# Moving the scaled input rows one block ahead and loading two sums one product sooner, in a two-layer encoder

## The chip, the core and the metric

The kernel runs on one core of one Trainium2 chip. A core has five engines that run side by side, each through its own list of instructions in order: TensorE (PE) multiplies matrices, VectorE (DVE) and ScalarE (ACT) work on tiles element by element, GpSimd (POOL) does a little arithmetic and issues DMAs, and SyncE (SP) only issues DMAs. DMAs move tiles between DRAM and the on-chip memory; those that add onto what is there already are issued by POOL here. The metric is the device time of one execution in microseconds (us); less is better. Times are medians of several executions.

## The reference

One sequence of 512 tokens of width 2048 goes through two layers in float32: attention with 16 query heads and 4 key/value heads, and a retention layer with 8 heads. What matters here are the large products with the weights and the residual.

```python
ALPHA = (2.0 * DEPTH) ** 0.25

def attention_mixer(h, w_in, q_gain, k_gain, w_out, cos, sin):
    proj = h @ w_in
    q, k, v, g = jnp.split(proj, [A_WIDTH, A_WIDTH + A_KV_WIDTH, A_WIDTH + 2 * A_KV_WIDTH], axis=-1)
    ...
    return (o * jax.nn.silu(g)) @ w_out

def retention_mixer(h, w_in, decay_exp, w_out, cos, sin):
    proj = h @ w_in
    q, k, v, g = jnp.split(proj, [R_QK_WIDTH, 2 * R_QK_WIDTH, 2 * R_QK_WIDTH + R_V_WIDTH], axis=-1)
    ...
    return (o * jax.nn.silu(g)) @ w_out

def reference(x, ...):
    for i in range(DEPTH):
        ...
        x = layer_norm(ALPHA * x + y, ln_gain[i], ln_bias[i])
    return x
```

## The kernel before

**Products.** A float32 product is made of three passes (`mm3`, L266 to L270): each operand is split into a rounded part and a remainder, and hi x hi, hi x lo and lo x hi are summed in PSUM. Weights come as chunks of 128 x 1024 values. One function, `split` (L116), makes the parts of a chunk: a cast on ACT (`whi`) and a subtraction on DVE (`wlo`). One chunk feeds twelve matmuls of 128 x 512 in the input blocks.

**Blocks.** The input projection of a layer is cut into blocks of 1024 columns, five in layer 1 (`a_in[0]` to `a_in[4]`, written block 0 to block 4 here) and twelve in layer 2 (`r_in`). Each block is a 2 x 2 product by Strassen's scheme, with seven products instead of eight; their numbers are 1 to 7, and the usual order is `ORDER` = 1, 5, 6, 3, 7, 2, 4. The weight side is cut into quarters B11, B12, B21, B22, and each product takes one sum of them, four chunks long. Those sums are formed in the raw tiles: `fetch` (L165) issues the load of a quarter on SP, `onto` (L145) adds another quarter by a DMA of POOL, and `make` (L183) adds two tiles on DVE: B22 for product 6 (L187), B21 for product 4 (L189). Product 5 needs B11 + B12. In an ordinary block that sum grows in the tile of product 1: once the chunk of product 1 is split, `follow` lets POOL add B12 onto it. In the blocks marked `first` (0 and 1 of each layer) products 1 and 2 stand far ahead, so `fetch` loads B11 again for product 5 and POOL adds B12.

**Order.** The first three blocks of a layer are interleaved as `LAYER_SEQ` says (block 0 products 1, 2; block 1 products 1, 2; block 0 products 5, 6, 3, 7; block 1 product 5; block 0 product 4; block 1 products 6, 3, 7; block 2 product 1; block 1 product 4; block 2 products 5, 6, 3, 7, 2, 4), then the others follow one by one. PE runs in exactly the order in which the code is written. The other engines' lists are put in order by the compiler's scheduler, except where `in_turn` ties instructions down. Chunks are split `AHEAD` = 2 ahead of PE and fetched `FETCH` = 3 ahead of that. A `hook` calls a function when PE's code reaches a given chunk of a given product of a block.

**Buffers.** Raw chunks live in a pool of 9 tiles (`rp`), and a load waits on SP until one is free. Split parts have 3 tiles each. A second pool, `xp`, has 32 tiles of the same size for the features, their sums and split forms, attention's operands and whatever needs a large buffer for long (`raw_load(..., large=True)`).

**Scaled rows.** The residual ALPHA * x goes into a DRAM tensor `yD`, onto which the output projection adds later. `residual_1` (L672 to L681) handles an eighth of it: SP loads 128 x 1024 values of x into an `xp` tile (L675), three chunks later ACT multiplies by ALPHA (L678) and POOL writes the tile to `yD` (L679). Its eight hooks stand in block 3 of layer 1 (L683 to L685), one in each of the seven products and a second in the fourth, product 3. Block 4 runs partly beside the start of attention, which reads keys, values, queries and gates back from DRAM.

Of the kernel before, what the change touches and what calls it, by code (L numbers as in the profile page):

```python
# [16 lines left out]
NT = S // P  # L17
# [26 lines left out]
ORDER = (1, 5, 6, 3, 7, 2, 4)  # L44

PAIR_SEQ = ((0, (1, 2, 5, 6, 3, 7)), (1, (1,)), (0, (4,)), (1, (5, 6, 3, 7, 2, 4)))
LAYER_SEQ = ((0, (1, 2)), (1, (1, 2)), (0, (5, 6, 3, 7)), (1, (5,)), (0, (4,)), (1, (6, 3, 7)), (2, (1,)), (1, (4,)),
             (2, (5, 6, 3, 7, 2, 4)))
# [5 lines left out]
def encoder_trunk_kernel(  # L54
# [33 lines left out]
    def nm(s):  # L88
        n_names[0] += 1
        return f"{s}{n_names[0]}"  # L90
# [4 lines left out]
    def x4(name, dt=F32R):  # L95
        return xp.tile([P, 1024], dt, tag="x", name=nm(name))
# [29 lines left out]
    def raw_load(src, large=False):  # L126
        raw = x4("raw", F32) if large else rp.tile([P, CH], F32, tag="raw", name=nm("raw"))
        x = nc.sync.dma_start(out=raw, in_=src)
        if fetched[0] < 12:
            in_turn(x)  # L130
        return raw

    def in_turn(x):

        tc.keep_in_program_order(x)
# [8 lines left out]
    def onto(x, src):  # L144
        return nc.gpsimd.dma_start(out=x, in_=src, accum_op=ALU.add)  # L145

    class Block:
# [17 lines left out]
        def fetch(self, p, c):  # L165
            q = lambda n: self.quarter(n, c)
            g = self.got
            if p == 1:
                g[1 if self.first else "v", c] = raw_load(q(11), self.hold)
            elif p == 2:  # L170
                g[2, c] = raw_load(q(21))
            elif p == 6:
                g[3, c] = raw_load(q(22), self.wide)
            elif p == 4 and self.again:
                g[2, c] = raw_load(q(21))
            elif p == 5 and self.first:
                if self.hold:
                    g["v", c] = g[1, c]
                else:
                    g["v", c] = raw_load(q(11))  # L180
                    onto(g["v", c], q(12))

        def make(self, p, c):  # L183

# [189 lines left out]
    def hook(blk, p, c, fn, *args):  # L374
        blk.hooks.setdefault((p, c), []).append(lambda: fn(*args))
# [150 lines left out]
    a_in = [Block(a["wa_in"][g], g < 2, hold=g == 0, again=g == 0, lean=g == A_G - 1) for g in range(A_G)]  # L526
    r_in = [Block(a["wr_in"][g], g < 2, again=g == 0) for g in range(R_G)]
# [47 lines left out]
    def form_hooks(ins, op):  # L575
        for (b, p, c), what in FORMS:
            hook(ins[b], p, c, op.form, *what)
# [102 lines left out]

        soon(3, scaled)  # L681

    for t in range(NT):  # L683
        for i in range(2):
            hook(a_in[3], ORDER[t + 3 * i], 1 + i, residual_1, t, i)  # L685

    cosq, sinq = [half(tabs, i).rearrange("p (t e) -> p t e", t=NT) for i in range(2)]

# [552 lines left out]
                x2.form(5, m // 2 % 2)  # L1241
    form_hooks(r_in, x2)
    hook(r_in[1], 6, 0, paused.clear)
    work.drain()


# [109 lines left out]
```

## Time and profile before

| what | value |
|---|---|
| median of 3 runs | 2105.22 us (2104.43 to 2105.92) |
| the profiled execution, its own time | 2108.04 us |
| its span from first to last instruction | 2106.2 us |
| granted clock of PE, mean | 0.998 |
| DMA, mean over the span | 186 GB/s, 390.80 MB |
| ACT, casts of `whi` (L117) | 644.7 us, 616 times |
| DVE, subtractions of `wlo` (L117) | 749.8 us, 616 times |
| SP waiting to load raw chunks (L128) until DVE has subtracted `wlo` | 524.6 us, 170 times |

In the profile, "out<-in" names the tile that an instruction writes and those that it reads; `raw` is a raw chunk, `acc` a sum in PSUM, `xs` a tile of scaled rows. "<-DVE wlo L117" at the end of a row says that the engine sat idle before it and that this ended the wait. PEld is the loading of weights into PE. A row of the chain of waits gives start, duration and what took the time; a DMA's duration runs from its issue to its landing. SP's rows are issues only: where two are merged, the duration runs from the first to the last.

### The profile page before, as it was taken

The page shows a single profiled execution, that of the slowest core. Times are in us where ns is not written, and L with a number is a line of the kernel's source. Part 1 is how long each engine was busy: PE and PEld are TensorE (multiplying, and loading weights), DVE is VectorE, ACT ScalarE, POOL GpSimd, SP SyncE. Part 2 cuts the span into 40 slices and gives each one's busy share as a digit, 9 for nine tenths or more (in the row PEclk, how much of TensorE's full clock was granted, in tenths as well). Part 3 has the DMA queues.
Part 4 walks back from the last instruction along what each step waited for, and adds up shares of the span by engine and source line. Part 5 has one row for each costly group of instructions (what it writes and reads, how often), then busy time and mean ns, then how long its engine had stood idle before and what let it go on. Part 6 is the DMA issues. An engine that isn't in the chain of part 4 may idle for free.

```text
span 2106.2 us, 26560 instructions
## 1 busy us (share of the span) xinstructions
PE 2084.9 (99%) x9684; PEld 1726.7 (82%) x9684; DVE 1611.2 (76%) x2153; ACT 1131.3 (54%) x1498; POOL 419.7 (20%) x507
## 2 busy tenths in 40 slices
PE   9999999999999999999999999999999999999997
PEld 7888887888888877888888888888888888888886
DVE  7888877889777878667786686666687888879666
ACT  6555556667643744444444444544466665666432
POOL 1144222122211112111211211211111122222100
PEclk9999999999999999999999999999999999999999
DMA  9776778457685868586786766566675587877762
GB/s 346 202 166 155 244 226 221 130 173 153 144 210 162 254 144 228 134 250 168 167 238 190 174 186 183 127 176 184 143 203 147 174 196 192 189 186 178 201 197 80
DMA packets 121971, 390.80 MB, mean 186 GB/s; under 512 B 14832, under 2 KB 17904, under 8 KB 121840
## 3 DMA queue, kind: packets, MB, share of 16 engines
q0 software_dynamic: 51040, 164.65, 38.0%
q1 hardware_dynamic: 70368, 223.53, 31.6%
q8 instruction: 76, 1.25, 0.2%
q10 hardware_dynamic: 432, 0.92, 0.1%
q14 instruction: 55, 0.45, 0.1%
HBM read 319.84 MB, written 69.21 MB: 185 GB/s over the span
## 4 chain that ended last, share of the span: by engine, by line
PE 88%; DVE 4%; DMA 4%; issue 2%; POOL 1%; ACT 1%; POOLq 0%; DVEq 0%; ACTq 0%
PE acc L269 25%; PE acc L270 25%; PE acc L268 25%; PE tr L522 3%; PE o L268 2%; PE o L269 2%; PE o L270 2%; PE s L268 1%; PE s L270 1%; PE s L269 1%; DVE wlo L117 1%; DMA raw<-in_wr_p_dram 1%; DMA raw<-in_wr_in_dram 1%; DMA raw<-in_wa_in_dram 1%; ACT whi L117 1%
## 5 line engine op out<-in xcount | busy, mean ns | idle before, releaser
L117 DVE TENSOR_TENSOR wlo<-raw,whi 128x1024 fp32r<-128x1024 f32 (+1 forms) x616 | 749.8, 1219 | 366.6 <-ACT whi L117 362.7
L117 ACT CAST whi<-raw 128x1024 fp32r<-128x1024 f32 (+1 forms) x616 | 644.7, 1050 | 665.5 <-PE acc L270 507.8
L268 PE MATMUL acc<-whi,f 128*128 128x512 f32 x2456 | 967.5, 394 | 1.5 <-ACT whi L117 1.5
L269 PE MATMUL acc<-wlo,f 128*128 128x512 f32 x2456 | 958.0, 390 | 6.6 <-DVE wlo L117 6.3
L270 PE MATMUL acc<-whi,f 128*128 128x512 f32 x2456 | 957.6, 390 | 0.0
L269 PEld LDWEIGHTS acc<-wlo,f 128*128 128x128 f32 x2456 | 461.7, 188 | 103.3 <-DVE wlo L117 12.0
L270 PEld LDWEIGHTS acc<-whi,f 128*128 128x128 f32 x2456 | 461.0, 188 | 96.9
L268 PEld LDWEIGHTS acc<-whi,f 128*128 128x128 f32 x2456 | 461.5, 188 | 94.6 <-ACT whi L117 3.0
L145 POOL DMA_DIRECT2D raw<-in_wr_in_dram x100 | 88.0, 880 | 396.4 <-DVE wlo L117 258.0
L187 DVE TENSOR_TENSOR raw<-raw,raw 128x1024 f32<-128x1024 f32 x86 | 105.1, 1227 | 2.3 <-DMA raw<-in_wa_in_dram 0.8
L386 ACT COPY t<-acc 128x512 f32<-128x512 f32 x150 | 84.8, 588 | 39.0 <-PE acc L270 35.0
L189 DVE TENSOR_TENSOR raw<-raw,raw 128x1024 f32<-128x1024 f32 x68 | 82.6, 1217 | 3.6 <-DMA raw<-in_wr_in_dram 3.6
L117 DVE TENSOR_TENSOR f<-xf,f 128x1024 fp32r<-128x1024 f32 (+2 forms) x67 | 78.1, 1171 | 9.1 <-ACT f L117 9.1
L117 ACT CAST f<-xf 128x1024 fp32r<-128x1024 f32 (+2 forms) x67 | 67.4, 1012 | 22.7 <-DMA xf<-in_xq_dram 5.8
L505 POOL TENSOR_TENSOR rstd<-rs_e,neg_half 128x1 f32<-128x1 f32 x40 | 31.3, 783 | 239.5 <-DVE rs_e L504 238.5
L145 POOL DMA_DIRECT2D raw<-in_wa_in_dram x48 | 42.7, 890 | 141.6 <-DVE wlo L117 111.3
L145 POOL DMA_DIRECT2D yD<-t x48 | 43.1, 986 | 117.9 <-DVE t L397 36.9
L1152 ACT ACTIVATE o<-o,nmr,rstd 128x512 f32<-128x512 f32 x32 | 24.9, 779 | 61.1 <-DVE nmr L516 61.1
L815 ACT ACTIVATE p<-s,nmax 128x512 f32<-128x512 f32 x64 | 44.1, 690 | 22.0 <-DVE s L813 17.1
L813 DVE TENSOR_SCALAR_CACHE_REDUCE s<-s,q_rs 128x512 f32<-128x512 f32 x64 | 48.0, 751 | 6.7 <-PE s L270 6.4
L268 PE MATMUL o<-inh,pTh 128*128 128x512 f32 x128 | 51.4, 401 | 0.0
L270 PE MATMUL o<-inh,pTl 128*128 128x512 f32 x128 | 50.0, 391 | 0.0
(205 smaller groups left out, 2200.0 us busy)
## 6 DMA issues: line engine op xcount, KB each, us to landing
raw<-in_wr_in_dram SPq DMA_DIRECT2D x156, 512.0 KB, 5.0
raw<-in_wr_in_dram POOLq DMA_DIRECT2D x100, 512.0 KB, 6.4
raw<-in_wa_in_dram SPq DMA_DIRECT2D x66, 512.0 KB, 6.2
raw<-in_wa_in_dram POOLq DMA_DIRECT2D x48, 512.0 KB, 7.6
raw<-in_wr_p_dram SPq DMA_DIRECT2D x36, 512.0 KB, 4.9
yD<-t POOLq DMA_DIRECT2D x48, 256.0 KB, 6.9
raw<-in_wr_p_dram POOLq DMA_DIRECT2D x24, 512.0 KB, 7.6
y<-yD SPq DMA_DIRECT2D x16, 512.0 KB, 6.5
```

The lines of the kernel that those rows point to most:

```text
L117: x, y = nc.scalar.copy(hi, src), nc.vector.tensor_sub(lo, src, hi.bitcast(F32))
L145: return nc.gpsimd.dma_start(out=x, in_=src, accum_op=ALU.add)
L187: nc.vector.tensor_add(v, v, g[3, c])
L189: x = nc.vector.tensor_add(v, v, g[2, c])
L268: nc.tensor.matmul(ps, sh, mh, start=start, stop=False, skip_group_check=go_on)
L269: nc.tensor.matmul(ps, sh, ml, start=False, stop=False, skip_group_check=go_on)
L270: nc.tensor.matmul(ps, sl, mh, start=False, stop=stop, skip_group_check=go_on)
L386: nc.scalar.copy(keep[p, t], bk[CHAIN[p]][t])
L505: nc.gpsimd.tensor_tensor(out=dst, in0=e[:, :n], in1=neg_half[:, :n], op=ALU.pow)
L522: nc.tensor.transpose(out=b[:, tcols(i)], in_=src[:, tcols(i)], identity=ident)
L813: nc.vector.tensor_scalar(sb, sb, rs, None, op0=ALU.mult, op1=ALU.min, accum_out=nmax)
L815: nc.scalar.activation(pt, sb, AF.Exp, scale=-1.0, bias=nmax, accum_out=self.sm[t][:, h:h + 1])
```

## The change

The first part hangs the eight calls of `residual_1` on block 2 of layer 1 (its last six products, 24 chunks, a call every third chunk) and no longer on block 3. The second part gives the load of B11 and the add of B12 for product 5 a function of its own, which does nothing where the sum is already asked for, and calls it for chunks 0 and 1 of layer 2's block 1 at the first two chunks of block 0's product 6, with large buffers out of `xp`.

```diff
@@ -177,8 +177,12 @@
                 if self.hold:
                     g["v", c] = g[1, c]
                 else:
-                    g["v", c] = raw_load(q(11))
-                    onto(g["v", c], q(12))
+                    self.fetch_sum(c)
+
+        def fetch_sum(self, c, large=False):
+            if ("v", c) not in self.got:
+                self.got["v", c] = raw_load(self.quarter(11, c), large)
+                onto(self.got["v", c], self.quarter(12, c))
 
@@ -680,9 +684,9 @@
-    for t in range(NT):
-        for i in range(2):
-            hook(a_in[3], ORDER[t + 3 * i], 1 + i, residual_1, t, i)
+    slots = [(p, c) for p in LAYER_SEQ[-1][1] for c in range(4)]
+    for n in range(2 * NT):
+        hook(a_in[2], *slots[3 * n], residual_1, n % NT, n // NT)
 
@@ -1241,6 +1245,8 @@
     hook(r_in[1], 6, 0, paused.clear)
+    for c in range(2):
+        hook(r_in[0], 6, c, r_in[1].fetch_sum, c, True)
     work.drain()
```

The number of instructions of every kind stays, and PE's list stays as it is. Source lines behind L178 move down by four, at the very end by six. Three places show what moves.

On POOL, at the head of block 4 of layer 1: the raw tiles are block 4's first four chunks, onto which B12 is added, `gD` and `qD` take gates and queries of block 3. Before:

```order
L679 DMA yD<-xs_2554 128x1024
L776 DMA qD_89<-qkT_2641 128x512
L505 TENSOR_TENSOR q_rs<-rs_e_2677,neg_half 128x4
L145 DMA raw_2581<-in_wa_in_dram 128x1024
L145 DMA raw_2611<-in_wa_in_dram 128x1024
L769 DMA gD_93<-gt_2711 128x512
L769 DMA gD_93<-gt_2714 128x512
L776 DMA qD_89<-qkT_2724 128x512
L145 DMA raw_2634<-in_wa_in_dram 128x1024
L679 DMA yD<-xs_2673 128x1024
L145 DMA raw_2666<-in_wa_in_dram 128x1024
```

and now:

```order
L780 DMA qD_89<-qkT_2645 128x512
L509 TENSOR_TENSOR q_rs<-rs_e_2679,neg_half 128x4
L145 DMA raw_2587<-in_wa_in_dram 128x1024
L145 DMA raw_2617<-in_wa_in_dram 128x1024
L773 DMA gD_93<-gt_2713 128x512
L773 DMA gD_93<-gt_2716 128x512
L780 DMA qD_89<-qkT_2726 128x512
L145 DMA raw_2638<-in_wa_in_dram 128x1024
L145 DMA raw_2670<-in_wa_in_dram 128x1024
```

The seventh and eighth write of scaled rows no longer stand ahead of and between the four adds.

On SP, in block 2 of layer 1: the first four raw tiles are its chunks of B22, those behind them its B21 for product 2. Before, no load of x stood here; the first came eight loads further on. Now:

```order
L128 DMA raw_1481<-in_wa_in_dram 128x1024
L128 DMA raw_1512<-in_wa_in_dram 128x1024
L679 DMA xs_1518<-in_x_dram 128x1024
L128 DMA raw_1537<-in_wa_in_dram 128x1024
L128 DMA raw_1557<-in_wa_in_dram 128x1024
L679 DMA xs_1596<-in_x_dram 128x1024
L679 DMA xs_1675<-in_x_dram 128x1024
L679 DMA xs_1750<-in_x_dram 128x1024
L128 DMA raw_1780<-in_wa_in_dram 128x1024
L128 DMA raw_1810<-in_wa_in_dram 128x1024
L679 DMA xs_1816<-in_x_dram 128x1024
L128 DMA raw_1834<-in_wa_in_dram 128x1024
```

Four loads of x go out among the chunks of B22, and the fifth stands between the second and third chunk of B21; it takes the buffer of the first, and so waits until that one's write has landed.

On DVE, where layer 2 goes from block 1's product 5 to block 0's product 4: rows of L189 add B21 for block 0's product 4 (`raw_6765`, `raw_6795`, `raw_6814`, `raw_6838` are its chunks 0 to 3), rows of L187 add B22 for block 1's product 6, and the `wlo` rows split a chunk. Before:

```order
L393 TENSOR_TENSOR t_6968<-t_6968,acc_6452 128x512
L189 TENSOR_TENSOR raw_6765<-raw_6765,raw_7190 128x1024
L117 TENSOR_TENSOR wlo_7217<-raw_7148,whi_7216 128x1024
L117 TENSOR_TENSOR wlo_7235<-raw_7167,whi_7234 128x1024
L189 TENSOR_TENSOR raw_6795<-raw_6795,raw_7214 128x1024
L117 TENSOR_TENSOR wlo_7254<-raw_6765,whi_7253 128x1024
L117 TENSOR_TENSOR wlo_7273<-raw_6795,whi_7272 128x1024
L189 TENSOR_TENSOR raw_6814<-raw_6814,raw_7232 128x1024
L189 TENSOR_TENSOR raw_6838<-raw_6838,raw_7250 128x1024
L117 TENSOR_TENSOR wlo_7296<-raw_6814,whi_7295 128x1024
```

and now (L193 and L191 are the old L189 and L187):

```order
L193 TENSOR_TENSOR raw_6765<-raw_6765,raw_7190 128x1024
L117 TENSOR_TENSOR wlo_7217<-raw_7148,whi_7216 128x1024
L193 TENSOR_TENSOR raw_6795<-raw_6795,raw_7214 128x1024
L117 TENSOR_TENSOR wlo_7235<-raw_7167,whi_7234 128x1024
L193 TENSOR_TENSOR raw_6814<-raw_6814,raw_7232 128x1024
L117 TENSOR_TENSOR wlo_7254<-raw_6765,whi_7253 128x1024
L193 TENSOR_TENSOR raw_6838<-raw_6838,raw_7250 128x1024
L191 TENSOR_TENSOR raw_6975<-raw_6975,raw_7269 128x1024
L117 TENSOR_TENSOR wlo_7273<-raw_6795,whi_7272 128x1024
L191 TENSOR_TENSOR raw_6995<-raw_6995,raw_7292 128x1024
L191 TENSOR_TENSOR raw_7148<-raw_7148,raw_7311 128x1024
L117 TENSOR_TENSOR wlo_7296<-raw_6814,whi_7295 128x1024
```

The additions of B21 for chunks 1 to 3 stand one or two places sooner, between the splits, and three additions of B22 now stand ahead of the split of chunk 2 of product 4 (`wlo_7296`). On POOL, the adds onto the two large buffers and onto chunk 2 of the sum (`raw_7148`) stand ahead of block 0's four adds for product 7; only chunk 3's stands behind them.

## The prediction

> **What bounds the kernel.** The order of views was: the page, PE's timeline, the chain of waits, the windows, then the timelines of SP and POOL and their waits.
>
> ```profile
> span 2106.2 us, 26560 instructions
> PE 2084.9 (99%) x9684; PEld 1726.7 (82%) x9684; DVE 1611.2 (76%) x2153; ACT 1131.3 (54%) x1498; POOL 419.7 (20%) x507
> ```
>
> PE is busy all the time, and the change leaves its instructions and their order as they are. So the only time to win is where PE stands still for operands, and the only time to lose is a new such place. I went through PE's timeline for starts that lie further apart than usual. Two groups hold most of what is lost after the start-up. The first is at the head of block 4 of layer 1:
>
> ```profile
> 337.19 0.39 PE L270 MATMUL acc<-whi,f 128*128 128x512 f32 x1
> 337.42 0.45 PE L268 MATMUL acc<-whi,f 128*128 128x512 f32 x1
> ...
> 338.97 0.39 PE L270 MATMUL acc<-whi,f 128*128 128x512 f32 x1
> ...
> 341.04 0.39 PE L270 MATMUL acc<-whi,f 128*128 128x512 f32 x1
> 342.50 0.50 PE L268 MATMUL acc<-whi,f 128*128 128x512 f32 x1 [1.07 <-ACT whi L117]
> 343.76 0.50 PE L269 MATMUL acc<-wlo,f 128*128 128x512 f32 x1 [0.76 <-DVE wlo L117]
> 344.10 0.40 PE L270 MATMUL acc<-whi,f 128*128 128x512 f32 x1
> ```
>
> The usual step from start to start is 0.23 (337.19 to 337.42). I count starts, since the ends are modelled. 337.42 to 338.97 are two steps that took 1.55 instead of 0.45, so 1.10 is lost; 341.04 to 342.50 loses 1.46 - 0.23 = 1.23; 342.50 to 344.10 loses 1.60 - 0.45 = 1.15. Together **3.48 us**. The second group is where layer 2 goes from its block 1, product 5, to block 0, product 4:
>
> ```profile
> 787.55 0.39 PE L270 MATMUL acc<-whi,f 128*128 128x512 f32 x1
> 788.35 0.50 PE L268 MATMUL acc<-whi,f 128*128 128x512 f32 x1 [0.41 <-ACT whi L117]
> ...
> 789.95 0.40 PE L270 MATMUL acc<-whi,f 128*128 128x512 f32 x1
> ...
> 800.78 0.39 PE L268 MATMUL acc<-whi,f 128*128 128x512 f32 x1
> 803.03 0.50 PE L269 MATMUL acc<-wlo,f 128*128 128x512 f32 x1 [1.87 <-DVE wlo L117]
> 803.37 0.39 PE L270 MATMUL acc<-whi,f 128*128 128x512 f32 x1
> ```
>
> Here 0.80 - 0.23 = 0.57, 1.60 - 0.45 = 1.15 and 2.59 - 0.45 = 2.14 are lost, together **3.86 us**. Both groups wait for a split whose raw chunk came late; the chain of waits says why.
>
> ```profile
> 326.16 15.14 DMA raw<-in_wa_in_dram
> ```
>
> **Part 1, the scaled rows.** The add of B12 into block 4's fourth chunk takes 15.14 us and lands at 341.30; PE gets the cast at 342.50 and the remainder at 343.76. The table of windows (busy us by engine, then granted clock, DMA share, GB/s) says why it takes so long:
>
> ```profile
> 300.00:305.00 5.00, 5.00 (x26) 4.13 (x25) 5.00 (x6) 2.96 (x4) 0.65 (x2) 1.00 0.45 150
> 305.00:310.00 5.00, 5.00 (x24) 4.13 (x23) 5.00 (x7) 2.19 (x3) 0.49 (x1) 1.00 0.95 302
> ...
> 335.00:340.00 5.00, 4.23 (x19) 3.14 (x18) 2.61 (x3) 1.57 (x2) 0.00 (x0) 1.00 1.04 302
> ```
>
> The 16 DMA engines are full from 305 to 340, so whatever leaves this stretch lets all that stands behind it land earlier by its service time. Three transfers of the scaled rows are in it, the eighth load and the last two writes (timelines of SP and POOL); the page's queue lines follow.
>
> ```profile
> 306.75 0.49 SPq L675 DMA_DIRECT2D xs<-in_x_dram  x1
> 314.63 0.54 POOL L679 DMA_DIRECT2D yD<-xs  x1
> ...
> 324.27 1.18 POOL L679 DMA_DIRECT2D yD<-xs  x1
> ```
>
> ```profile
> q0 software_dynamic: 51040, 164.65, 38.0%
> q1 hardware_dynamic: 70368, 223.53, 31.6%
> ```
>
> The queue lines give the service time of 512 KB (0.524 MB). On SP's queue it is 0.316 x 2106.2 x 0.524 / 223.53 = 1.56 us. On POOL's, mostly adds, it is 2.55 us; a plain write has no row of its own, so I bound it by these two. Sum: 1.56 + 2 x (1.56 to 2.55) = 4.7 to 6.7 us off the backlog. What is needed: without stall the chunk's second matmul would start at 341.04 - 1.10 + 2 x 0.23 = 340.4. It started at 343.76, so the landing has to come 3.4 us sooner, and 4.7 covers that. The chunk before needs 1.0 us, which the write at 314.63 gives alone. After it the attention's matmuls spread the chunks out, so nothing is near. I take 3.4 of the 3.48.
>
> The Trainium skill (DMA: Bandwidth & Descriptors, Queues, rings and completion order) says that each DMA engine takes turns between the queue rows, packet by packet. By it the load on SP's queue would delay POOL's adds by less than its service, and the two writes alone would count in full. The sum would then be 3.1 to 5.1 us against the 3.4 needed, and up to 0.3 of stall would stay. The 15.14 us of an add in a full stretch agrees with shared engines, but no row here separates the two queues' turns.
>
> The work itself is not saved. Eight loads, eight multiplies and eight writes now run in block 2. What covers them (SP's timeline, the windows, the multiply's own line):
>
> ```profile
> 169.36 0.33 SPq L128 DMA_DIRECT2D raw<-in_wa_in_dram  x1
> ```
>
> ```profile
> 170.00:180.00 10.00, 10.00 (x48) 8.31 (x47) 10.00 (x14) 6.17 (x8) 5.60 (x2) 1.00 0.25 90
> ...
> 200.00:210.00 10.00, 10.00 (x48) 8.28 (x47) 5.77 (x7) 5.01 (x6) 2.19 (x3) 1.00 1.03 215
> 210.00:220.00 10.00, 10.00 (x46) 8.29 (x45) 9.73 (x17) 4.39 (x6) 2.26 (x2) 1.00 0.53 186
> ```
>
> ```profile
> L678 ACT ACTIVATE xs<-xs x8: 1047/1057/1073, 252.6 to 322.2; 128x1024 f32<-128x1024 f32 x8
> ```
>
> In SP's new order the first load stands behind block 2's second chunk of B22 and three more behind the fourth, which goes out at 169.36; all four have a free buffer. Three of them thus fall into the window with a share of 0.25, and their 4.7 us fill it less than half. A multiply takes 1.06 us of ACT, which idles 4 to 6 us in ten here, and there is one in three chunks. The fifth to seventh load and the third to fifth write meet 200 to 220, full in its first half and half free in its second: 3 x 1.56 + 3 x (1.56 to 2.55) = 9.4 to 12.3 us of service against 4.7 free there. What does not fit, up to 7.6 us, moves on behind 220, where five of these loads no longer come. Chunks may land a few us later, but PE waits nowhere in this stretch now (10.00 of 10 in these rows). I price it at 0, and at rival (d) if the cover fails.
>
> **Part 2, B11 + B12 sooner.** The chain there:
>
> ```profile
> 774.64 7.55 DMA raw<-in_wr_in_dram
> ...
> 784.59 1.20 DVE t L393 x2
> 785.78 1.15 DVE raw L189
> ...
> 786.94 6.05 DMA raw<-in_wr_in_dram
> ...
> 795.41 5.19 DMA raw<-in_wr_in_dram
> ```
>
> Two things are late. First the adds of B12, of which the one at 774.64 is the second chunk's: these give the 0.57 and 1.15. Second, behind them, the loads of B21 for block 0's product 4: they need a raw buffer, and one is freed only when DVE has added the one before (L189, 785.78), so load and addition alternate until the last addition lets the split go that PE gets at 803.03 (the 2.14). With two chunks in large buffers the first changes at once: their loads need only a buffer that PE's transposes of the layer norm gave up.
>
> ```profile
> 734.35 0.33 SPq L128 DMA_DIRECT2D raw<-in_wr_in_dram  x1
> ```
>
> ```profile
> 745.00:755.00 10.00, 10.00 (x46) 8.29 (x45) 10.00 (x10) 5.74 (x7) 0.00 (x0) 1.00 0.00 0
> ```
>
> Their loads should go out right behind the one at 734.35, and their adds are done before 755, where the DMA share is 0.00 now; this costs nothing. The third chunk's load takes the place the first had. The fourth goes one freed buffer earlier, one chunk time of 12 x 0.23 = 2.7 us, and off the crowded stretch. So all four sums should be there before PE's turn: 1.72 us saved.
>
> For the second: the loads of B21 for chunks 0 to 2 now find free buffers as product 7 gives them up; only chunk 3 waits for L189. Product 7's last matmul is two chunks before the one at 787.55, at 787.55 - 2 x 2.7 = 782.1; L393 twice (1.20) and L189 (1.15), no longer held until 784.59, then end near 785.0 instead of 786.9, and chunk 3's load lands at 785.0 + 5.19 to 6.05 = 790.2 to 791.1 instead of 800.6. What is late next is the row of additions of B22 (L187) that DVE's new order puts ahead of the split: their loads go out as L189 and a split free buffers, at about 787.3, 789.6 and 790.8. The third lands at 796.0 to 796.9; addition and split (1.15 to 1.2 each) end at 798.4 to 799.3. PE, rid of 1.72, wants that split at 800.78 - 1.72 + 0.23 = 799.3 and, rid of smaller steps too, some tenths sooner. So 0 to 0.4 stays; I take 0.2. Part 2 gives 3.86 - 0.2 = 3.66, about 3.7.
>
> **Sum.** 3.4 + 3.7 = 7.1 us of the profiled execution (2108.0 us, 2.8 above the median). The stalls are no property of that one run, so I take them off the median: 2105.2 - 7.1 = **2098.1 us**.
>
> **Rivals.**
> (a) The backlog at 305 to 340 shrinks too little: only the last write, 1.56 us, counts for the late add. Then 3.4 - 1.56 = 1.8 stays: 2099.9. For it: the load and the first write were issued 19 and 12 us before the add. Against: the windows show no pause in between.
> (b) The buffers go on alternating and the 2.14 stays, as if a load took ten us: 2100.2. Against: the load moves by ten.
> (c) The change doesn't do what it says: the adds stay late because POOL or DMA fills the same way elsewhere, under 1 us is won: 2105.
> (d) Slower: SP blocks. In block 3 the fifth load waited 25.1 us for a write to free its buffer (SP's waits):
>
> ```profile
> SPq L675 <- DMA yD<-xs: 25.1, 1, 25.1
> ```
>
> ```profile
> 207.73 0.33 SPq L128 DMA_DIRECT2D raw<-in_wa_in_dram  x1
> ```
>
> ```profile
> 180.42 0.58 ACT L773 COPY qkT<-tr 128x512 f32<-128x512 f32 x1
> ```
>
> ```profile
> DMA to landing us min/median/max: 2.9/7.3/13.8
> ```
>
> In block 2 it comes behind the load at 207.73, ahead of two of product 2's loads and of block 3's. SP asks for a chunk five chunks ahead of PE (AHEAD + FETCH), 13.6 us, of which landing, cast and split take some 7.5 by the rows above. So SP may stand there until about 217; each us beyond costs one. Blocked for 25.1 us, to 233, it costs 16: 2105.2 - 7.1 + 16 = 2114. The change turns into a loss from 224 on. Against: the first write now follows its multiply, which stands right behind the copy at 180.42, and even with the slowest landing, 13.8, it is there by 196.
>
> **How the numbers follow.** Forecast 0.58 (2097.1 to 2099.5), (a) 0.14, (b) 0.10, (c) 0.11, (d) 0.07. The low end is the full 7.34 off, less the half span of the three runs (0.75). The high end, 2102.5, takes in (a) and (b) with twice their remainder; left out are (c) and (d), 0.18. A measurement of this kernel can tell 0.2%, 4.2 us, from no change: faster than 2101.0 are the forecast and most of (a) and (b), 0.76; slower 0.07; the rest 0.17.
>
> **What would show it.** Right: no gap over 0.3 us on PE around 335 to 345; the add that took 15.14 us lands in under 12; the eight loads between 162 and 230 with no SP wait of 10 us; two loads near 735; the first L189 about 2 us sooner, its last about 9. Wrong: a PE gap between 165 and 260, an ACT wait at the multiply, or a new wait for L187 where L189's was.

## The result, and the profile after

The changed kernel takes **2099.16 us** (median of 7 runs, 2098.53 to 2101.55). The kernel before, run beside it, takes 2105.78 us (7 runs, 2104.43 to 2108.82). The ratio is **0.9973, interval 0.9964 to 0.9982**: 5.7 us less, between 3.8 and 7.6. (The two medians lie 6.6 apart, which is inside that interval.)

The page of the changed kernel (busy us, share of the span, instructions):

```profile
span 2098.7 us, 26552 instructions
PE 2083.2 (99%) x9684; PEld 1726.7 (82%) x9684; DVE 1611.3 (77%) x2153; ACT 1133.2 (54%) x1498; POOL 419.5 (20%) x507
```

The span is 7.5 us shorter (2106.2 before), with the same 9684 matmuls. PE's timeline at the head of block 4 of layer 1 (start, duration, engine, line, operation), first before, then after:

```profile
334.70 0.39 PE L268 MATMUL acc<-whi,f 128*128 128x512 f32 x1
...
351.16 0.39 PE L268 MATMUL acc<-whi,f 128*128 128x512 f32 x1
```

```profile
334.70 0.39 PE L272 MATMUL acc<-whi,f 128*128 128x512 f32 x1
...
337.42 0.39 PE L272 MATMUL acc<-whi,f 128*128 128x512 f32 x1
337.65 0.41 PE L273 MATMUL acc<-wlo,f 128*128 128x512 f32 x1
...
340.22 0.39 PE L272 MATMUL acc<-whi,f 128*128 128x512 f32 x1
340.56 0.50 PE L273 MATMUL acc<-wlo,f 128*128 128x512 f32 x1
...
347.98 0.39 PE L272 MATMUL acc<-whi,f 128*128 128x512 f32 x1
```

Both pieces run from the first matmul of product 5's second chunk to the first of product 6's second. 57 steps lie between, and 334.70 to 337.42 gives 2.72 / 12 = 0.2267 for a step, so 12.92 us without a stall. Before it took 16.46, after 13.28: the **loss went from 3.54 to 0.36 us**, and no step is over 0.35 us. I use this "loss at block 4" for every run below.

In layer 2, from the first chunk of block 1's product 5 to the second of its product 6, 108 steps or 24.48 us without a stall, before and after:

```profile
782.34 0.39 PE L268 MATMUL acc<-whi,f 128*128 128x512 f32 x1
...
811.34 0.39 PE L268 MATMUL acc<-whi,f 128*128 128x512 f32 x1
```

```profile
779.26 0.39 PE L272 MATMUL acc<-whi,f 128*128 128x512 f32 x1
...
803.74 0.39 PE L272 MATMUL acc<-whi,f 128*128 128x512 f32 x1
```

29.00 before, 24.48 after: the **loss in layer 2 went from 4.52 to 0**. Together that is 3.18 + 4.52 = 7.7 us. Some of it was given back elsewhere, in block 6 of layer 2 (ACT's timeline, the two kernels after one another; a bracket names the wait that ended):

```profile
1181.50 2.01 ACT L117 CAST whi<-raw 128x1024 fp32r<-128x1024 f32 x2 [1.95 <-DMA raw<-in_wr_in_dram]
```

```profile
1175.05 2.94 ACT L117 CAST whi<-raw 128x1024 fp32r<-128x1024 f32 x3 [3.72 <-DMA raw<-in_wr_in_dram]
```

PE is 7.7 us ahead there, but this cast only 6.45 (1181.50 to 1175.05). PE had no time to spare at it before and lost 0.05 us in the six chunks around it; after, it lost 1.37. The change touches nothing in that block; the last section comes back to it.

### The profile page after: what moved, and what is told of

Its sections match the earlier page's. It is cut to its first block, busy times and chain, and to the rows that moved or that the text cites. A ratio compares the mean times of both kernels' runs of the same rounds, so it can differ in the third digit from the quotient of the medians.

```text
span 2098.7 us, 26552 instructions
## 1 busy us (share of the span) xinstructions
PE 2083.2 (99%) x9684; PEld 1726.7 (82%) x9684; DVE 1611.3 (77%) x2153; ACT 1133.2 (54%) x1498; POOL 419.5 (20%) x507
## 4 chain that ended last, share of the span: by engine, by line
PE 78%; issue 12%; DVE 3%; DMA 3%; POOL 2%; ACT 1%; POOLq 0%; DVEq 0%; SPq 0%; ACTq 0%
PE acc L273 22%; PE acc L274 22%; PE acc L272 22%; PE tr L526 3%; PE o L272 2%; PE o L274 2%; PE o L273 2%; DMA raw<-in_wr_p_dram 1%; PE s L272 1%; PE s L274 1%; PE s L273 1%; DVE wlo L117 1%; POOL raw L145 1%; ACT whi L117 1%; DMA raw<-in_wr_in_dram 1%
## 5 line engine op out<-in xcount | busy, mean ns | idle before, releaser
L191 DVE TENSOR_TENSOR raw<-raw,raw 128x1024 f32<-128x1024 f32 x86 | 105.3, 1228 | 3.1 <-DMA raw<-in_wa_in_dram 1.7
L193 DVE TENSOR_TENSOR raw<-raw,raw 128x1024 f32<-128x1024 f32 x68 | 82.6, 1217 | 0.0
L1078 POOL DMA_DIRECT2D qkD<-qkT x32 | 24.3, 759 | 131.0 <-ACT qkT L1076 130.6
```

Source lines behind the costliest of these rows:

```text
L191: nc.vector.tensor_add(v, v, g[3, c])
L193: x = nc.vector.tensor_add(v, v, g[2, c])
```

## The experiments

Times are medians, ratios are against runs of the kernel before on the same chip (medians there 2105.55 to 2106.66). "Cast" is ACT's cast of block 4's fourth chunk (the one behind the add that took 15.14 us), counted from PE's first matmul of the second chunk, so that runs whose PE is shifted can be compared.

| kernel | us | ratio (interval) | cast | loss at block 4 | loss in layer 2 |
|---|---|---|---|---|---|
| before | 2105.78 | | 6.70 | 3.54 | 4.52 |
| changed | 2099.16 | 0.9973 (0.9964 to 0.9982) | 3.29 | 0.36 | 0 |
| E1 rows alone | 2103.31 | 0.9984 (0.9975 to 0.9993) | 3.25 | 0.30 | 3.56 |
| E2 sums alone | 2103.51 | 0.9988 (0.9979 to 0.9997) | 5.38 | 3.81, 1.6 of it clock | 0 |
| E3 large, not sooner | 2106.28 | 0.9996 (0.9987 to 1.0005) | 6.69 | 3.55 | 0, and 2.24 ahead of it |
| E4 sooner, not large | 2106.42 | 1.0000 (0.9991 to 1.0008) | 5.75 | 4.20, 1.6 of it clock | 2.78 |
| E5 changed + load | 2099.57 | 0.9965 (0.9952 to 0.9978) | 3.89 | 0.75 | 0 |
| E6 changed + POOL write | 2100.95 | 0.9972 (0.9961 to 0.9984) | 4.60 | 1.45 | 0 |
| E7 changed + SP write | 2099.36 | 0.9962 (0.9947 to 0.9977) | 3.15 | 0.02 | 0 |
| E8 changed + all three | 2100.50 | 0.9972 (0.9959 to 0.9984) | 4.73 | 1.53 | 0 |
| E9 changed + thirteen | 2105.92 | 0.9996 (0.9987 to 1.0005) | 4.48 | 1.47 | 0 |
| E10 changed + sixteen | 2109.33 | 1.0012 (1.0003 to 1.0021) | 6.53 | 4.95, 1.6 of it clock | 0 |
| E11 residual moved | 2098.65 | 0.9961 (0.9949 to 0.9974) | 2.90 | 0 | 0 |
| E12 changed + four | 2098.31 | 0.9966 (0.9954 to 0.9979) | 3.00 | 0.01 | 0 |

Two cautions go with the table. First, in E2, E4 and E10 not all of the loss at block 4 is waiting. Right behind the stall PE's steps are 0.43 us instead of 0.23 for about 3.4 us, with no wait, and the granted clock (third number from the end of a row of windows) is below 1. PE's timeline of E2 and its windows:

```profile
343.51 0.63 PE L272 MATMUL acc<-whi,f 128*128 128x512 f32 x1
343.94 0.63 PE L273 MATMUL acc<-wlo,f 128*128 128x512 f32 x1
```

```profile
340.00:345.00 5.00, 3.42 (x10) 2.56 (x11) 4.11 (x5) 4.23 (x6) 0.14 (x1) 0.81 0.18 48
```

Eight steps of 0.43 cost 1.6 us over eight of 0.2267. So the waiting at block 4 is 2.2 us in E2, 2.6 in E4 and 3.35 in E10. Second, the profiles of kernels with the same first layer differ. With the rows in block 3, the cast is at 6.70 (before), 6.69 (E3), 5.38 (E2) and 5.75 (E4), and PE waits 3.54, 3.55, 2.2 and 2.6 us. With the rows in block 2 and nothing put back, the cast is at 3.29 (changed), 3.25 (E1) and 2.90 (E11). A difference of 0.4 us in this column says nothing.

### E1 and E2: each part alone

E1 is the changed kernel without its last hunk; E2 keeps the last hunk and the old hooks of the rows.

```
E1, taken out:
-    for c in range(2):
-        hook(r_in[0], 6, c, r_in[1].fetch_sum, c, True)
E2, put back:
+            hook(a_in[3], ORDER[t + 3 * i], 1 + i, residual_1, t, i)
```

> Part 1 alone: the scaled rows move to block 2 of layer 1, the sums of layer 2's block 1 are fetched as before. Theory (two separate stalls, each with its own cure): the steps at the head of block 4 (3.48 us lost before) shrink to 0.4 us or less, the three steps of layer 2 (0.57, 1.15 and 2.14) stay as they are, 3.9 us; the time is 3.2 us below before, about 2102.5. Rival (the two parts lean on each other, for instance because PE coming earlier into layer 2 opens the second stall wider): the second group loses 5 us or more and the time is within 2 us of before.

> Part 2 alone: the rows stay in block 3. Theory: the head of block 4 loses its 3.5 us as before (the add that took 15.14 us still takes 14 to 16), and the second group is gone, 0.3 us or less; the time is 4 to 4.5 us below before, about 2101.5. Rival (the second group was partly made by PE's phase after the first stall): over 1 us of it stays.

Measured: 0.16% (0.07 to 0.25) and 0.12% (0.03 to 0.21) below before, together 0.28%; the whole change has 0.27%. Each part cures its own stall and leaves the other, so the parts add up; with intervals this wide, that they do so to 0.01% is luck. The stall that is left is not quite the old one either: E1 still loses 3.56 of the 4.52 us in layer 2, and E2's 3.81 at block 4 is 2.2 of waiting and 1.6 of lower clock. In E2 block 4's add took 13.84 us, not 14 to 16.

### E3 and E4: is it the buffer or the earlier turn?

Both keep the rows where they were before.

```
E3:
+    r_in[1].large = 2
+                    self.fetch_sum(c, c < self.large)
E4:
+        hook(r_in[0], 6, c, r_in[1].fetch_sum, c)
```

> Rows as before; the two sums of layer 2's block 1 in large buffers, but asked for at product 5's usual turn. SP's order is then almost that of part 2, since a load that needs no raw buffer doesn't stand and wait; POOL's adds keep their usual place. Theory of the buffers (what counts is that two raw buffers are not tied up): the alternation of L189 and loads is gone, the 2.14 us goes, and so do the 0.57 and 1.15 if the loads leave near 735; 4 to 4.5 us below before. Rival (what counts is the earlier turn of the adds on POOL): the adds land near 782 and 787 as before, 0.57 and 1.15 stay, and 2.1 to 2.7 us are won.

> Rows as before; the two sums are asked for one product sooner, but in ordinary raw buffers. SP's order of loads and the waits for buffers stay those of before, only the adds of B12 move on POOL. Theory of the buffers: only the first chunk's load was out by 735 before, the second still waits for a raw buffer until about 768; the 2.14 us stays and at most the 0.57 goes: within 1 us of before. Rival (the earlier turn is what counts): 1.7 us or more are won, with both the 0.57 and the 1.15 gone.

Neither alone is clear of before. In E3 the loss in layer 2's counted piece is gone, as the theory of the buffers has it, but a new stall stands just ahead of it. POOL's timeline of E3, and ACT's:

```profile
760.99 2.63 POOL L145 DMA_DIRECT2D raw<-in_wr_in_dram  x3 [1.42 <-DVE wlo L117]
764.04 0.86 POOL L145 DMA_DIRECT2D raw<-in_wr_in_dram  x1 [0.42 <-DVE wlo L117]
766.31 0.89 POOL L145 DMA_DIRECT2D raw<-in_wr_in_dram  x1 [1.41 <-DVE wlo L117]
```

```profile
775.17 1.05 ACT L117 CAST whi<-raw 128x1024 fp32r<-128x1024 f32 x1 [5.07 <-DMA raw<-in_wr_in_dram]
779.73 2.94 ACT L117 CAST whi<-raw 128x1024 fp32r<-128x1024 f32 x3 [3.51 <-DMA raw<-in_wr_in_dram]
```

Block 0 has four adds of B12 for its product 7, each issued once a chunk of product 3 is split. The group of three is the second of these and two adds of the sums: with the buffers free, the sums' adds go out right behind 761, ahead of the last two for product 7 (764.04 and 766.31), instead of behind them. The chunks of product 7 that need those two are cast at 775.17 and 779.73, and PE loses 2.24 us there. In the changed kernel the same two adds are out long before:

```profile
739.21 0.86 POOL L145 DMA_DIRECT2D raw<-in_wr_in_dram  x1 [0.87 <-PE acc L274]
740.42 0.86 POOL L145 DMA_DIRECT2D raw<-in_wr_in_dram  x1 [0.35 <-issue]
```

They land by 749.1, and the DMA share is 0.00 from 750 to 755, before the first add for product 7 (755.50) goes out.

In E4 the second chunk's load still waits for a raw buffer until 769.8, as it did until 768.6 before, and its add goes out at 776.3. 2.78 us stay lost of 4.52, but E1, with this stretch unchanged, shows 3.56, so at most 0.8 of that is E4's doing. So the large buffers let the loads go early and free the two raw buffers; the earlier turn is what puts the adds ahead of those for product 7. Both are needed.

### E5 to E8: the three transfers, put back one by one

The changed kernel gets transfers of 512 KB that nobody reads, at the places that the scaled rows had. E8 has the load and two writes.

```
+    def extra_load():
+        in_turn(nc.sync.dma_start(out=x4("xs", F32), in_=a["x"][3][:, 1024:2048]))
+    def extra_write(queue, n):
+        in_turn(queue.dma_start(out=scratch[:, n], in_=tabs))
E5: +    hook(a_in[3], 4, 2, extra_load)
E6: +    hook(a_in[3], 4, 2, soon, 3, extra_write, nc.gpsimd, 1)
E7: as E6 on nc.sync, behind the split of that place
E8: E5 + E6 + hook(a_in[3], 2, 2, soon, 3, extra_write, nc.gpsimd, 0)
```

> The changed kernel, and beside it one more load of 512 KB on SP's queue at the place in SP's order where the kernel before had the eighth load of scaled rows (near 306 us); nobody reads it. In the changed kernel the late add lands at 337.9, 11.75 us after its issue. Theory (the 16 DMA engines are one shared backlog; only a pause between can swallow a transfer): from 315 to 325 the share is 0.89 and 0.91, so about 1 us of pause swallows most of the load's 1.56 us; the add lands 0 to 1 us later, the head of block 4 loses 0 to 1 us more. Rival (the backlog is full all the way, as the prediction had it): 1.5 us or more later, and as much lost.

> The changed kernel, and beside it one more write of 512 KB (of a table, to scratch) on POOL's queue at the place of the last write of scaled rows (near 324 us, right ahead of the late add). Theory of the backlog: nothing swallows it, the add lands 1.6 to 2.6 us later, at 339.5 to 340.5, and the head of block 4 loses as much more than in the changed kernel. Rival (it was not the queue, but the multiplies or the buffers of the scaled rows that made the stall): no change.

> The same extra write of 512 KB, but on SP's queue, at a place near 314 us. Theory of one shared backlog: it counts like a transfer on POOL's queue, less what the pause from 315 to 325 swallows: the add lands 0.5 to 1.6 us later. Rival (each DMA engine takes turns between the queues, so what stands on SP's queue costs POOL's adds little): under 0.4 us later.

> The changed kernel with three extra transfers at the three places that the scaled rows had (load near 306 on SP's queue, writes near 314 and 324 on POOL's). Nothing waits for them. Theory of the backlog: the stall comes back as it was before, the add takes 14 to 16 us, and the head of block 4 loses 3 to 3.5 us; the time is 3 us above the changed kernel. Rival (the stall needed the waits and buffers of the scaled rows as well): under 1.5 us comes back.

The chain of waits, one row each from E5, E6 and E8 (start, duration of the late add):

```profile
326.28 12.36 DMA raw<-in_wa_in_dram
```

```profile
326.44 12.91 DMA raw<-in_wa_in_dram
```

```profile
326.60 13.06 DMA raw<-in_wa_in_dram
```

By the cast, the load costs 0.60, the last write 1.31 (the theory wanted 1.6 to 2.6), the SP write nothing that could be told (-0.14), and all three 1.44 instead of 3.4. The load and the first write in E8 thus cost 0.13 on top of the last write, whichever queue they are on: a transfer that is early enough adds next to nothing. The windows of the changed kernel (DMA share and GB/s last) show some room between, which the kernel before, with 1.03 and 1.04 there, didn't have:

```profile
315.00:320.00 5.00, 5.00 (x24) 4.14 (x23) 4.04 (x7) 2.40 (x3) 2.08 (x2) 1.00 0.89 282
320.00:325.00 5.00, 5.00 (x26) 4.14 (x25) 1.61 (x2) 3.33 (x5) 3.45 (x5) 1.00 0.91 173
```

That they were taken up there is likely, but not shown. E8's expectation fell: the three transfers are 1.2 of the 3.2 us of loss that left. The rest had another source.

### E9, E10 and E12: the rest of the rows

What else differed was already there before 305: in the kernel before, block 3's last chunks were cast and split late, and so block 4's first add was issued at 319.49; in the changed kernel it was 317.85, and in E8 318.06. E9 puts back seven loads and six writes (all but the three), E10 all sixteen, E12 only the two writes and two loads that stood between 286 and 291. The code is E9's, and the comments say what differs in the others.

```
+    for n, place in enumerate(places):
+        if n < 7:                              # E10: 8, E12: n in (5, 6)
+            hook(a_in[3], *place, extra_load)
+        if n < 6:                              # E10: 8, E12: n in (3, 4)
+            hook(a_in[3], *place, soon, 3, extra_write, n)
```

> The changed kernel with extra transfers (512 KB each, nobody reads or waits for them) at the places in block 3 that the scaled rows had, but for the last three: seven loads on SP's queue and six writes on POOL's, the last of them near 300 us. The three of 306, 314 and 324 us are left out. Open after the run with those three: they brought back only 1.2 of the 3.2 us. Theory (lag): the two loads and two writes between 286 and 291 made the raw chunks of block 3's last products late; each later load waits for the buffer of an earlier split, so the lag of 1.5 to 2 us stays until block 4's adds are issued. Then the splits of block 3's last product leave PE about 1 us instead of the 2.7 to 3.2 of the changed kernel, and the head of block 4 loses 1 to 2 us with none of the three transfers there. Rival (the lag has nothing to do with it, the rest is the multiplies on ACT or chance): the splits stay 2.5 us or more ahead and at most 0.5 us is lost.

> The same with all eight loads and eight writes as extra transfers in their old places, without the multiplies. Theory (lag and the last three transfers add up): 3 to 3.6 us are lost at the head of block 4, as before the change, and the time is about 3 us above the changed kernel. Rival (multiplies on ACT, or the wait of 25.1 us for a buffer): 1.2 to 2 us.

> The changed kernel with only four extra transfers of 512 KB: two loads and two writes at the places in block 3 that the kernel before had between 286 and 291 us. (In the run with thirteen extra transfers 6.5 us were lost at the head of block 3 already, so what it shows of the lag is mixed with that.) Theory (lag): PE loses nothing in block 3, the splits of its last product leave PE 1 to 2 us instead of 2.7 to 3.2, block 4's first add is issued about 1 us later than in the changed kernel, measured from PE's block start, and the head of block 4 loses 0.8 to 2 us. Rival (the backlog of 305 to 340 alone counts): the lag is gone by 305, and the head of block 4 loses 0.5 us or less.

E9 loses 1.47 at block 4 with none of the three transfers, and DVE's splits of block 3's last product lead PE by 1.7 to 2.3 us only (2.8 to 3.4 in the changed kernel). E10, with everything back but the multiplies and the rows' own waits, loses 4.95, of which 3.35 is waiting, as much as was expected. So transfers alone make the stall, and those ahead of 305 have a share. But E9 and E10 also lose 6.5 and 8.3 us at the head of block 3, where the changed kernel's own last rows still are. About 2 us of each is lower clock again (0.61 from 260 to 265 in E9, 0.50 from 265 to 270 in E10). So their size, and their time, say little. PE's timeline of E9 there:

```profile
262.02 0.80 PE L272 MATMUL acc<-whi,f 128*128 128x512 f32 x1 [3.01 <-ACT whi L117]
263.28 0.79 PE L273 MATMUL acc<-wlo,f 128*128 128x512 f32 x1 [0.46 <-DVE wlo L117]
```

E12 was to separate that, and its theory fell: no lag, no loss at block 4. POOL's and ACT's timelines, one behind the other for each kernel, say why the four transfers weren't it. Before:

```profile
275.74 0.90 POOL L145 DMA_DIRECT2D raw<-in_wa_in_dram  x1 [1.70 <-DVE wlo L117]
276.35 0.85 POOL L679 DMA_DIRECT2D yD<-xs  x1
278.94 0.86 POOL L145 DMA_DIRECT2D raw<-in_wa_in_dram  x1 [1.73 <-DVE wlo L117]
281.25 0.86 POOL L145 DMA_DIRECT2D raw<-in_wa_in_dram  x1 [1.46 <-DVE wlo L117]
```

```profile
291.52 2.00 ACT L117 CAST whi<-raw 128x1024 fp32r<-128x1024 f32 x2 [0.94 <-DMA raw<-in_wa_in_dram]
```

E12, the same two views:

```profile
281.40 0.87 POOL L145 DMA_DIRECT2D raw<-in_wa_in_dram  x1 [1.45 <-DVE wlo L117]
281.94 1.43 POOL L697 DMA_DIRECT2D scratch<-tabs  x2
```

```profile
289.64 1.06 ACT L117 CAST whi<-raw 128x1024 fp32r<-128x1024 f32 x1 [0.66 <-ACT r_sq L728]
```

E9, the same two views:

```profile
282.32 0.88 POOL L697 DMA_DIRECT2D scratch<-tabs  x1
285.04 0.85 POOL L145 DMA_DIRECT2D raw<-in_wa_in_dram  x1 [1.84 <-DVE wlo L117]
```

```profile
296.74 1.05 ACT L117 CAST whi<-raw 128x1024 fp32r<-128x1024 f32 x1 [1.06 <-DMA raw<-in_wa_in_dram]
```

Before, one write (276.35) stood between the second and the third of block 3's four adds of B12 for product 7. The fourth add, issued at 281.25, landed at 291.4; the cast of 291.52 waited for it. In E9 a write stands at the same place, and the same cast waits for the DMA. In E12 the writes stand behind the fourth add, and the cast waits for no DMA. So the late start of block 4's adds goes with that write ahead of two adds.

All the profiles together bear this out, and give the two shares. The fourth add's time to landing, in the kernel before, in E2 and in the changed kernel (one transfer each, so the three figures agree):

```profile
DMA to landing us min/median/max: 10.2/10.2/10.2
```

```profile
DMA to landing us min/median/max: 9.1/9.1/9.1
```

```profile
DMA to landing us min/median/max: 5.9/5.9/5.9
```

"Lag" is how much later than in the changed kernel the splits of block 3's last product are, measured from PE and averaged over the four chunks. The three transfers are put at E8's 1.44 wherever they are there.

| kernel | the write ahead of two adds | fourth add | lag | three transfers | lag + transfers | cast later than in changed |
|---|---|---|---|---|---|---|
| before | yes | 10.2 | 1.8 | 1.4 | 3.2 | 3.41 |
| E3 | yes | 10.1 | 1.7 | 1.4 | 3.1 | 3.40 |
| E10 | yes | 9.6 | 1.2 | 1.4 | 2.6 | 3.24 |
| E9 | yes | 9.4 | 1.1 | 0 | 1.1 | 1.19 |
| E2 | yes | 9.1 | 0.8 | 1.4 | 2.2 | 2.09 |
| E4 | yes | 8.9 | 0.6 | 1.4 | 2.0 | 2.46 |
| E8 | no | 5.9 | 0 | 1.4 | 1.4 | 1.44 |
| E12 | no | 6.3 | 0 | 0 | 0 | -0.29 |

The slower the fourth add, the larger the lag, and lag plus transfers give the cast to within 0.7 us. The same first layer has a lag of 1.8 in one profile and 0.6 in another, so the share of the three transfers is anything from two fifths (before) to two thirds (E2) of the gain. The write wasn't put back by itself; that it is the cause is read from these traces, not shown by a run that changes it alone.

### E11: a version that might be faster

Block 6 of layer 2 lost 1.37 us in the changed kernel. E11 hooks layer 2's residual rows to other blocks.

```
-            hook(r_in[3 + c], (1, 6, 3, 2)[t], 0, load_residual, c, t)
+            hook(r_in[(4, 5, 7, 8)[c]], (1, 6, 3, 2)[t], 0, load_residual, c, t)
```

> A version that might beat the changed kernel: layer 2's residual rows (load of normed rows, scale, write) are hooked to blocks 4, 5, 7 and 8 instead of 3, 4, 5 and 6, so that none follows directly on a block of gates (2, 5). In block 6 the adds of B12 share the DMA queues with them and with the gates of block 5: 0 to 2.2 us were lost there from execution to execution (1.3 in the changed kernel's profile, none before). Theory: this loss goes to under 0.2 us and the 0.3 at block 3 goes too; the time is 0.5 to 1.5 us below the changed kernel. Rival: the crowding moves along to blocks 7 and 8, no gain.

Block 6 loses nothing in E11, and its 2098.65 us (ratio 0.9961, 0.9949 to 0.9974) is the time of the changed kernel within the intervals. But E9, E10 and E12, with the old hooks, lose nothing in block 6 either. So it isn't shown that E11 is a gain.

## Why the prediction held, point by point

**What bounds it: right.** Matmuls and their order stayed, and the two stalls named are the two that went.

**Part 1, size right, make-up wrong.** Predicted 3.4 us; measured 3.18 of 3.54 (E1 alone 3.24). "The add that took 15.14 us lands in under 12" was met: it is issued at 326.14, and the cast that waits for it starts at 337.99 (ACT's timeline of the changed kernel), 3.41 us sooner than before (341.40) where 3.4 were needed:

```profile
337.99 1.05 ACT L117 CAST whi<-raw 128x1024 fp32r<-128x1024 f32 x1 [1.22 <-DMA raw<-in_wa_in_dram]
```

The step that failed is the sum "4.7 to 6.7 us off the backlog": the three transfers, put back, move the cast by 1.44 us of the 3.41 that it had gained (6.70 to 3.29). The step took DMA shares from 0.93 to 1.08 for a queue that never pauses; the two earlier transfers cost next to nothing. Of its rivals, (a) was right about the transfers (only the last write counts: 1.31 measured, 1.56 supposed) and wrong about the time, since it didn't see the other 2 us either. By the table above those go with block 3's chunks being on time again, which the prediction didn't price at all. That the size came out is luck in a second way: with the same rows in the same place, E2 and E4 wait 2.2 and 2.6 us there and not 3.5.

The rule that it cited (the Trainium skill, DMA: Bandwidth & Descriptors, Queues, rings and completion order: engines take turns between queues) isn't decided here. The write on SP's queue cost nothing (E7), but the early write on POOL's queue cost nothing either (E8), so place explains it without the queue.

**The moved rows, right, and nearer the edge than it reads.** Priced at 0: the stretch from block 1's product 4 (third chunk) to block 3's product 6 takes 96.51 us before and 96.48 after. Rival (d) did not happen: the fifth load goes out at 205.47 with no wait, and the eight lie between 162.94 and 226.13 as foretold (SP's timeline of the changed kernel):

```profile
162.94 0.86 SPq L679 DMA_DIRECT2D xs<-in_x_dram  x1
...
205.47 0.49 SPq L679 DMA_DIRECT2D xs<-in_x_dram  x1
...
226.13 0.76 SPq L679 DMA_DIRECT2D xs<-in_x_dram  x1
```

The cover was used up, though. DVE's split of the first chunk of block 2's product 2 and PE's first use of it (DVE's and PE's timelines), before and then after:

```profile
215.53 1.21 DVE L117 TENSOR_TENSOR wlo<-raw,whi 128x1024 fp32r<-128x1024 f32 x1
```

```profile
219.27 0.39 PE L268 MATMUL acc<-whi,f 128*128 128x512 f32 x1
```

```profile
217.22 1.22 DVE L117 TENSOR_TENSOR wlo<-raw,whi 128x1024 fp32r<-128x1024 f32 x1
```

```profile
219.32 0.39 PE L272 MATMUL acc<-whi,f 128*128 128x512 f32 x1
```

2.5 us of lead have become 0.9.

**Part 2, mechanism right, size as near as the profiles can tell.** Predicted 3.66; measured 4.52, and 4.52 in E2 alone. But E1, with this stretch as before, loses 3.56 there, so the stall itself is anything from 3.6 to 4.5 us. For the profile that the prediction worked from, two terms were off. Steps below half a us weren't counted: 4.52 by chunk starts against 3.86 by the large steps. And 0.2 us were left for the last split; it ended early enough (DVE's timeline of the changed kernel):

```profile
780.16 1.22 DVE L193 TENSOR_TENSOR raw<-raw,raw 128x1024 f32<-128x1024 f32 x1
...
787.46 1.22 DVE L193 TENSOR_TENSOR raw<-raw,raw 128x1024 f32<-128x1024 f32 x1
...
793.23 1.22 DVE L117 TENSOR_TENSOR wlo<-raw,whi 128x1024 fp32r<-128x1024 f32 x1
```

On this clock PE is 3.1 us ahead (782.34 to 779.26). The first B21 add, at 780.16 instead of 785.78, is 2.5 us sooner beside it (about 2 foretold), and the last split ends at 794.45 + 3.1 = 797.5 where 798.4 to 799.3 was worked out. The prediction took 5.19 to 6.05 us for a load from the crowded trace, for chunk 3's B21 and again for B22; they landed 4.0 and 3.6 to 4.6 us after issue. Rival (b) did not happen: the four additions of B21, which alternated with loads before, stand 2.3 to 2.8 us apart. That part 2 rests on large buffers and on the earlier turn, E3 and E4 show.

**The sum.** 7.1 foretold, 7.5 between the profiled spans, 5.7 (3.8 to 7.6) by the runs. The profiled spans agree partly by luck: 7.7 from the two places, less 1.32 in block 6, plus small steps elsewhere that come and go.

## What to carry to other kernels

A DMA share near 1 is no proof that a transfer taken out moves everything behind it: here only the one right ahead of the late add counted nearly in full, and the rest of the gain came with chunks that had been late since 35 us earlier. A stall that one profile shows has a size of its own in the next; profile the unchanged kernel more than once before pricing it. Before moving a fetch, ask both where its buffer is freed and what it will stand in front of on the issuing queue; either half of part 2 alone gained nothing that could be measured. A copy of a suspected transfer that nobody reads prices it in its place, and can show that the place you blamed holds only part of the loss. Before a late start on PE is called a wait, read the granted clock beside it.

## What the runs showed of the hardware that wasn't expected

Block 6 of layer 2 runs the same instructions in all kernels but E11, yet in the 13 others the loss there (six chunks, 16.32 us without a stall) was 0.05 in the kernel before, 1.37 in the changed one, 0 in E1, E4, E9, E10 and E12, 1.73 and 2.23 in E6 and E7, and between these in the rest. The chain of the changed kernel names an add of B12:

```profile
1162.55 12.41 DMA raw<-in_wr_in_dram
```

An add in a crowded stretch thus takes a us or two more or less in one execution than in another, and where chunks come with no lead PE pays that. One profile each can't attribute a difference of 1 us to an edit; the place has to be looked at in several.

The granted clock fell behind some stalls and not behind others. It is 0.81 and 0.85 in the two windows from 340 to 350 in E2, 0.87 and 0.79 there in E4, and 0.78 and 0.88 from 350 to 360 in E10, each time while PE takes 0.43 us for a step. In the kernel before and in E3, whose waits at the same place are longer than those of E2 and E4, it is 1.00 in every window from 325 to 360. What sets it off isn't shown here; at block 4 it costs 1.6 us each time.
